# Where the weight sums of the token mixing are added: accumulating DMAs or VectorE

## The chip, the cores and the metric

The kernel runs on one core of a Trainium2 chip. The metric is device time in microseconds of one execution; the time before is the median of three runs. The engines named below are TensorE (PE in the profile, PEld for its weight loads), VectorE (DVE), ScalarE (ACT), GpSimd (POOL) and SyncE (SP), the last of which issues most DMAs.

## What is computed

One decoder layer on 512 tokens of width 1024, all in float32. Three sub-layers, each between RMS norms, with a residual:

```python
h = h + 0.5 * rmsnorm(swiglu(rmsnorm(h, ffn1_pre_w), ffn1_w_gu, ffn1_w_down), ffn1_post_w)
u = rmsnorm(h, mix_pre_w)
y = token_mixing(u, mem, w_in, ...)          # three branches, gated and summed, then w_out
h = h + rmsnorm(y, mix_post_w)
h = h + 0.5 * rmsnorm(swiglu(rmsnorm(h, ffn2_pre_w), ffn2_w_gu, ffn2_w_down), ffn2_post_w)
```

The token mixing projects u with w_in (1024 x 10240). Its columns feed a gated linear recurrence in chunks of 64 tokens (4 heads), a dilated sliding-window attention (3 groups of 4 heads), a cross-attention into 256 memory tokens (4 heads) and the gates of these three branches. Each branch's output goes through a 512 x 1024 matrix, is multiplied by its gate, and the sum goes through w_out.

## The kernel before

All of a stage's activations stay on the chip; the weights stream in from memory, and each is split into a high and a low float32r part (`wsplit`, `split`): ScalarE copies the high part (L161), VectorE subtracts it to get the low one (`tt`, L158). A product is then three matmuls: high by high, high by low, low by high.

Two column tiles of 128 columns, c1 and c2, are projected together, as a *pair*: a 2 x 2 block product in Strassen's manner, with seven block products in place of eight. The blocks of the weights are quarters of 512 rows by 128 columns: a11 and a12 (upper and lower half of c1), a21 and a22 (of c2). `wops` gives the seven operands: a11, a12, a22 and four sums:

- s1 = a21 + a22 (operand 5)
- s2 = s1 + a11 (operand 6)
- s3 = a21 + a11 (operand 7)
- s4 = s2 + a12 (operand 3)

`pair` takes the products in the order 1, 6, 5, 7, 2, 3, 4: twelve matmuls of 256 columns for each, 84 in all. At j = 6 it asks for s4 and with it for s2 and s1. `pairs` calls `wops`, which issues the loads, one pair ahead.

Loads: `load` brings a11 and a12 into one tile `st` (512 KB, four buffers). a22 goes into a tile named `sh` (256 KB, two buffers). The sums live in five buffers with the tag `sum`. In the kernel before, s1 and s3 are made by DMAs: the quarter a21 is loaded twice, once into each of two `sum` tiles (SP, L151), and POOL then issues a DMA that adds a22 to the one and a11 to the other (L302). s2 and s4 are VectorE adds (L309, through `tt`, so that the profile has them at L158).

Where the mixing has pairs: `hgrn_pair` (three pairs each for hg0 and hg1), `dil_pair` (six each for dil0 and dil1), mq0 and mq1 (one each), and `branch` (four for each of three branches), 32 in all. `ORDER` lists its steps. The two feed-forward stages (`ffn`) have 20 pairs each.

Order: the Python program gives the order of the work; attention steps are generators that `tick` resumes after so many microseconds of matmuls by the table `LAT`. A scheduler in the framework then lays down, when the program is built, the order of the instructions on each engine and each queue and gives out the tiles' buffers. At run time every engine takes its queue in order. Loads by `fetch` keep the order of the program; loads by `bring` are placed by the scheduler outside the first stage.

Of the kernel before, what the change touches and what calls it, by code (L numbers as in the profile page):

```python
# [12 lines left out]
ALU = mybir.AluOpType  # L13
# [4 lines left out]
P = 128  # L18
# [4 lines left out]
DFF = 2816  # L23
NF = DFF // P
# [28 lines left out]
class Layer:  # L53
# [228 lines left out]
                out += [(hi[:, i, :], lo[:, i, :]) for i in range(per)]  # L282
        return out

    def wops(self, w, c1, c2):

        st = self.load(w, 0, KD, c1, P)
        a11, a12 = st[:, 0:4, :], st[:, 4:8, :]  # L290
        a22 = self.stage.tile([P, 4, P], F32, tag="st2", bufs=2, name=f"sh{self.uid()}")
        quarter = lambda h: w.rearrange("(k p) c -> p k c", p=P)[:, 4 * h:4 * h + 4, c2:c2 + P]
        self.bring(a22, quarter(1))
        sums, ops = {}, {}

        def new_sum():
            return self.wpool.tile([P, 4, P], F32, tag="sum", bufs=NSUM, name=f"sum{self.uid()}")

        for n, x in (("s1", a22), ("s3", a11)):
            u = new_sum()  # L300
            self.bring(u, quarter(0))
            self.nc.gpsimd.dma_start(out=u, in_=x, accum_op=ALU.add)  # L302
            sums[n] = u

        def total(n):
            if n not in sums:
                a, b = {"s2": ("s1", a11), "s4": ("s2", a12)}[n]
                u = new_sum()
                self.tt(u, total(a), b, ALU.add)  # L309
                sums[n] = u  # L310
            return sums[n]

        def get(j):
            if j not in ops:
                if j == 6:
                    total("s4")
                ops[j] = self.wsplit({1: a11, 2: a12, 4: a22}.get(j) if j in (1, 2, 4) else total({3: "s4", 5: "s1", 6: "s2", 7: "s3"}[j]))
            return ops[j]
        return get

    def pairs(self, specs):

        ahead = None
        for x in specs:
            now, ahead = ahead, self.wops(*x)
            if now:
                yield now
        yield ahead
# [84 lines left out]
    def ffn(self, w_gu, w_down, w_post, ready, reload, after, chunks, early, plain):  # L413
# [3 lines left out]
        y = [[self.slot() for _ in range(2)] for _ in range(NT)]  # L417
        gw = self.col_tiles(w_gu, 0, plain)
        uw = self.col_tiles(w_gu, DFF, plain)
        pairs = self.pairs([(w_gu, f * P, DFF + f * P) for f in range(plain, NF)])  # L420

        def swiglu(sg, su, act):
            nc.scalar.activation(sg, sg, AF.Silu)
# [54 lines left out]
        for n in chunks:  # L478
            act = []
            for j in range(n):  # L480
                if before and 2 * j % n == 0:
                    ws = []
                    for i in range(0, before[1], 2):
                        ws += down_weights(before[0] + i, 2 * j // n)
                if f0 + j < early:
                    act.append(heads[f0 + j][1])
                else:
                    act.append(new_act())
                    if f0 + j < plain:
                        gu_plain([self.wcol(next(g)) for g in (gw, uw)], act[-1], slice(0, T))  # L490
                    else:
                        gu(next(pairs), act[-1])
                if before:
                    for i in range(8 * j // n, 8 * (j + 1) // n):
                        down(i % NT, i // NT, before[2], ws, before[0] == 0)
            before = (f0, n, act)
            f0 += n
# [236 lines left out]
    def dil_values(self, hd, s0, s12, st0, st1, v, out):  # L734
# [44 lines left out]
        for s in (s0, s12):  # L779
            pTs = []  # L780
            for i in range(2):
                tp = self.paux((P, 4, P))
                lo = 1 if (s is s0 and i == 0) else 0
                for j in range(lo, 4):
                    self.transpose(tp[:, j, :], s[i][:, j // 2, j % 2, :])
                pT = self.slot((P, 4, P))
                if s is s0:
                    nc.scalar.copy(pT[:, lo:, :], tp[:, lo:, :])
                else:
                    nc.vector.tensor_copy(out=pT, in_=tp)  # L790
                pTs.append(pT)
            yield LAT['dil3']
            po = self.paux((P, 4, P))
            for b in range(4):
                pT, j = pTs[b // 2], 2 * (b % 2)
                if s is s0:
                    pairs = [(v[0][b - 1], pT[:, j, :])] if b > 0 else []
                    pairs.append((v[0][b], pT[:, j + 1, :]))
                else:
                    pairs = [(v[1][b], pT[:, j, :]), (v[2][b], pT[:, j + 1, :])]  # L800
                for n, (vv, pp) in enumerate(pairs):
                    self.mm(po[:, b, :], vv[:, hs], pp, n == 0, n == len(pairs) - 1)
            if s is s0:
                nc.scalar.copy(y, po.rearrange("p a b -> p (a b)"))
            else:
                yv = y.rearrange("p (s a) -> p s a", a=4)
                self.tt(yv, yv, po.rearrange("p a s -> p s a"), ALU.add)
# [300 lines left out]
```

## Time and profile before

| what | value |
|---|---|
| three timed runs | 1394.15 us median (1392.47 to 1395.41) |
| the profiled execution | 1396.16 us |
| its span in the trace | 1394.4 us |
| instructions in it | 24579 |
| TensorE, VectorE, ScalarE, GpSimd busy | 1341.6, 1016.6, 744.5, 161.8 us |

Times in the trace count from the span's start. The busy time of TensorE is that of pipelined matmuls, each with a modelled end, so that it is not TensorE at its peak. "Idle before, and what ended it" names the instruction or DMA whose signal came last; "issue" stands there where the profile shows no such signal. The granted clock is the share of TensorE's full clock of 2.4 GHz.

By the trace the first feed-forward stage lasts until about 350 us, the mixing until about 1010 us; from about 1050 us on it is the second feed-forward stage.

### The profile page before, as it was taken

How to read it: one execution, taken by the hardware profiler on the slowest of the kernel's cores; microseconds unless marked ns; L12 is line 12 of the kernel's file. 1: busy time of each engine (PE TensorE's matmuls, PEld its weight loads, DVE VectorE, ACT ScalarE, POOL GpSimd, SP SyncE). 2: the span in 40 equal slices, each digit the busy share in tenths (PEclk: the TensorE clock that was granted, in tenths of full speed). 3: DMA queues.
4: the chain of work that ended last, by engine and by line, in shares of the span. 5: the costliest groups of instructions: out<-in, count | busy, mean ns of one | idle time of the engine just before them, and what ended most of it. 6: DMA issues, size and time to landing. Idle time of an engine off the chain costs nothing.

```text
span 1394.4 us, 24579 instructions
## 1 busy us (share of the span) xinstructions
PE 1341.6 (96%) x9197; PEld 1242.3 (89%) x9197; DVE 1016.6 (73%) x1932; ACT 744.5 (53%) x1527; POOL 161.8 (12%) x204
## 2 busy tenths in 40 slices
PE   6999999999999699998899999999999999999997
PEld 6999999999788688898889899999889999999995
DVE  6887777776888574576777787787569777767765
ACT  6675545554576464353655555555457655445541
POOL 1011110110200100111201201110010100100000
PEclk9999999999999899999899999999999999999998
DMA  9676565656536534576456656665365776655513
GB/s 269 141 185 180 137 151 148 158 143 179 175 96 178 150 106 136 148 184 150 103 126 149 166 127 160 154 163 131 111 219 145 175 181 160 150 145 140 149 46 136
DMA packets 264238, 210.95 MB, mean 151 GB/s; under 512 B 10645, under 2 KB 216886, under 8 KB 264118
## 3 DMA queue, kind: packets, MB, share of 16 engines
q1 hardware_dynamic: 242870, 171.56, 41.6%
q0 software_dynamic: 21248, 37.82, 16.4%
q8 instruction: 72, 1.18, 0.4%
q14 instruction: 48, 0.39, 0.1%
HBM read 162.12 MB, written 9.47 MB: 123 GB/s over the span
## 4 chain that ended last, share of the span: by engine, by line
PE 46%; DVE 3%; issue 2%; DMA 2%; ACT 0%; POOL 0%; DVEq 0%; POOLq 0%; ACTq 0%
PE ps L354 9%; PE ps L355 9%; PE ps L353 9%; PE ps L334 3%; PE ps L333 3%; PE ps L335 3%; PE px L340 2%; PE px L333 2%; PE px L334 2%; PE px L335 2%; DVE s L158 1%; DVE w L158 1%; PE px L344 1%; DMA sh<-in_w_in_dram 1%; DMA sum<-sh 1%
## 5 line engine op out<-in xcount | busy, mean ns | idle before, releaser
L161 ACT ACTIVATE w<-sum 128x512 fp32r<-128x512 f32 x288 | 180.1, 631 | 222.1 <-PE ps L354 174.9
L158 DVE TENSOR_TENSOR w<-sum,w 128x512 fp32r<-128x512 f32 x288 | 196.6, 689 | 87.1 <-ACT w L161 85.5
L353 PE MATMUL ps<-xhi,w 128*128 128x256 f32 x864 | 247.4, 286 | 0.9 <-ACT s L371 0.9
L355 PE MATMUL ps<-xhi,w 128*128 128x256 f32 x864 | 246.0, 285 | 0.7 <-DVE w L158 0.7
L354 PE MATMUL ps<-xlo,w 128*128 128x256 f32 x864 | 245.5, 284 | 0.0
L161 ACT ACTIVATE w<-st 128x512 fp32r<-128x512 f32 x260 | 163.5, 630 | 137.4 <-PE ps L354 97.1
L158 DVE TENSOR_TENSOR w<-st,w 128x512 fp32r<-128x512 f32 x260 | 177.3, 689 | 34.0 <-ACT w L161 32.1
L158 DVE TENSOR_TENSOR s<-s,s 128x256 f32<-128x256 f32 (+3 forms) x316 | 177.2, 566 | 19.0 <-ACT s L161 4.2
L353 PEld LDWEIGHTS ps<-xhi,w 128*128 128x128 f32 x864 | 166.7, 193 | 3.5 <-ACT s L371 1.1
L354 PEld LDWEIGHTS ps<-xlo,w 128*128 128x128 f32 x864 | 166.5, 193 | 2.5 <-issue 0.2
L355 PEld LDWEIGHTS ps<-xhi,w 128*128 128x128 f32 x864 | 166.8, 193 | 0.9 <-DVE w L158 0.9
L302 POOL DMA_DIRECT2D sum<-st x72 | 62.7, 871 | 642.9 <-DVE s L158 374.9
L158 DVE TENSOR_TENSOR sum<-sum,st 128x512 f32<-128x512 f32 x144 | 99.3, 690 | 46.0 <-issue 34.9
L158 DVE TENSOR_TENSOR s<-s,ps 128x256 f32<-128x256 f32 (+1 forms) x194 | 92.5, 478 | 33.5 <-PE ps L335 25.0
L333 PE MATMUL px<-s,s 128*128 128x512 f32 x288 | 112.6, 391 | 0.0
L334 PE MATMUL px<-s,s 128*128 128x512 f32 x288 | 112.5, 391 | 0.0
L335 PE MATMUL px<-s,s 128*128 128x512 f32 x288 | 112.0, 389 | 0.0
L302 POOL DMA_DIRECT2D sum<-sh x72 | 63.6, 883 | 301.2 <-DMA sh<-in_w_in_dram 101.5
L353 PE MATMUL ps<-t3hi,w 128*128 128x256 f32 x288 | 83.3, 289 | 0.5 <-DVE s L158 0.5
L353 PE MATMUL ps<-t4hi,w 128*128 128x256 f32 x288 | 82.0, 285 | 0.8 <-ACT s L374 0.8
L354 PE MATMUL ps<-t3lo,w 128*128 128x256 f32 x288 | 82.5, 286 | 0.0
L353 PE MATMUL ps<-t2hi,w 128*128 128x256 f32 x288 | 82.4, 286 | 0.0
(185 smaller groups left out, 3433.4 us busy)
## 6 DMA issues: line engine op xcount, KB each, us to landing
st<-in_ffn_w_gu_dram SPq DMA_DIRECT2D x48, 512.0 KB, 4.8
st<-in_w_in_dram SPq DMA_DIRECT2D x48, 512.0 KB, 4.2
st<-in_ffn_w_down_dram SPq DMA_DIRECT2D x44, 512.0 KB, 3.9
sum<-in_ffn_w_gu_dram SPq DMA_DIRECT2D x80, 256.0 KB, 3.3
sum<-sh POOLq DMA_DIRECT2D x72, 256.0 KB, 3.8
sum<-st POOLq DMA_DIRECT2D x72, 256.0 KB, 3.8
sum<-in_w_in_dram SPq DMA_DIRECT2D x64, 256.0 KB, 3.2
sh<-in_ffn_w_gu_dram SPq DMA_DIRECT2D x40, 256.0 KB, 3.5
```

What stands on the lines that cost most here:

```text
L158: self.pin(self.nc.vector.tensor_tensor(out=out, in0=a, in1=b, op=op))
L161: self.pin(self.nc.scalar.activation(hi, src, AF.Copy))
L302: self.nc.gpsimd.dma_start(out=u, in_=x, accum_op=ALU.add)
L333: mm(out, lhsT=lhs[0], rhs=rhs[0], start=first, stop=False)
L334: mm(out, lhsT=lhs[0], rhs=rhs[1], start=False, stop=False)
L335: mm(out, lhsT=lhs[1], rhs=rhs[0], start=False, stop=last)
L340: self.nc.tensor.matmul(out, lhsT=lhsT, rhs=rhs, start=start, stop=stop, **k)
L344: self.nc.tensor.transpose(out, in_, self.ident)
L353: mm(out, lhsT=lh, rhs=rh, start=first and k == 0, stop=False, skip_group_check=True)
L354: mm(out, lhsT=lh, rhs=rl, start=False, stop=False, skip_group_check=True)
L355: mm(out, lhsT=ll, rhs=rh, start=False, stop=k == 3, skip_group_check=True)
```

## The change

In the mixing, a21 is loaded once. VectorE adds s1 = a21 + a22 into a new `sum` tile when s1 is first asked for (at j = 6, before s2 and s4), and s3 = a21 + a11 in place in a21's tile when s3 is asked for (at j = 7). The feed-forward stages keep the two loads and the two accumulating DMAs.

```diff
-    def wops(self, w, c1, c2):
+    def wops(self, w, c1, c2, by_load):
...
-        for n, x in (("s1", a22), ("s3", a11)):
-            u = new_sum()
-            self.bring(u, quarter(0))
-            self.nc.gpsimd.dma_start(out=u, in_=x, accum_op=ALU.add)
-            sums[n] = u
+        if by_load:
+            for n, x in (("s1", a22), ("s3", a11)):
+                u = new_sum()
+                self.bring(u, quarter(0))
+                self.nc.gpsimd.dma_start(out=u, in_=x, accum_op=ALU.add)
+                sums[n] = u
+        else:
+            a21 = sums["a21"] = new_sum()
+            self.bring(a21, quarter(0))
 
         def total(n):
+            if n == "s3" and n not in sums:
+                total("s1")
+                self.tt(a21, a21, a11, ALU.add)
+                sums[n] = a21
             if n not in sums:
-                a, b = {"s2": ("s1", a11), "s4": ("s2", a12)}[n]
+                a, b = {"s1": ("a21", a22), "s2": ("s1", a11), "s4": ("s2", a12)}[n]
                 u = new_sum()
                 self.tt(u, total(a), b, ALU.add)
                 sums[n] = u
...
-    def pairs(self, specs):
+    def pairs(self, specs, by_load=False):
...
-            now, ahead = ahead, self.wops(*x)
+            now, ahead = ahead, self.wops(*x, by_load)
...
-        pairs = self.pairs([(w_gu, f * P, DFF + f * P) for f in range(plain, NF)])
+        pairs = self.pairs([(w_gu, f * P, DFF + f * P) for f in range(plain, NF)], True)
```

## Rows read from the trace of the kernel before

**Rows 1.** First page, totals: busy us, share of the span, instructions

```profile
PE 1341.6 (96%) x9197; PEld 1242.3 (89%) x9197; DVE 1016.6 (73%) x1932; ACT 744.5 (53%) x1527; POOL 161.8 (12%) x204
```

**Rows 2.** Busy time by stretch: length, busy (instructions) per engine, clock, DMA share, GB/s

```profile
core 0: us, PE busy (x) PEld busy (x) DVE busy (x) ACT busy (x) POOL busy (x), PEclk, DMA share, GB/s
...
455.00:490.00 35.00, 23.21 (x168) 22.40 (x167) 20.92 (x46) 16.24 (x38) 3.58 (x6) 0.80 0.53 137
...
590.00:668.00 78.00, 71.18 (x562) 69.53 (x561) 55.28 (x116) 37.37 (x89) 12.60 (x16) 0.97 0.71 169
...
777.00:795.00 18.00, 15.38 (x113) 14.80 (x113) 15.65 (x32) 10.93 (x31) 3.91 (x5) 0.91 0.75 181
795.00:980.00 185.00, 185.00 (x1313) 174.31 (x1313) 145.29 (x290) 108.65 (x209) 19.82 (x24) 1.00 0.58 144
```

**Rows 3.** Timeline of TensorE, rows after a wait: start, length, instruction, [idle before, releaser]

```profile
415.14 0.39 PE L355 MATMUL ps<-xhi,w 128*128 128x256 f32 x1 [0.71 <-DVE w L158]
...
466.02 1.09 PE L344 MATMUL px<-ident,s 128*128 128x128 f32 x4 [6.74 <-DVE s L190]
...
664.32 2.04 PE L340 MATMUL px<-s,s 128*128 128x128 f32 x8 [4.93 <-DVE s L158]
...
683.45 1.71 PE L340 MATMUL px<-s,s 128*128 128x256 f32 x4 [2.21 <-ACT s L575]
...
780.61 1.16 PE L340 MATMUL px<-s,s 128*128 128x128 f32 x8 [0.50 <-DVE s L158]
```

**Rows 4.** Busy time by stretch, columns as in rows 2, where the clock was low

```profile
663.40:670.20 6.80, 5.88 (x27) 5.92 (x28) 3.39 (x8) 5.09 (x20) 2.12 (x3) 0.50 0.41 120
...
789.70:793.10 3.40, 3.23 (x15) 3.26 (x16) 1.17 (x4) 2.63 (x7) 1.87 (x4) 0.50 1.04 257
```

**Rows 5.** Timeline of VectorE, 645 to 661 us, end of the first dil stage

```profile
645.67 1.42 DVE L158 TENSOR_TENSOR sum<-sum,st 128x512 f32<-128x512 f32 x2 [3.82 <-issue]
...
649.88 0.68 DVE L158 TENSOR_TENSOR w<-sh,w 128x512 fp32r<-128x512 f32 x1
...
652.10 1.30 DVE L158 TENSOR_TENSOR w<-sum,w 128x512 fp32r<-128x512 f32 x2
...
653.63 0.69 DVE L158 TENSOR_TENSOR w<-sum,w 128x512 fp32r<-128x512 f32 x1
657.66 1.42 DVE L158 TENSOR_TENSOR sum<-sum,st 128x512 f32<-128x512 f32 x2 [3.34 <-issue]
...
660.27 1.27 DVE L738 TENSOR_REDUCE st<-s 128x2 f32<-128x512 f32 x2
```

**Rows 6.** The queues beside it: SP, POOL, and landing of `sh` in 590 to 668

```profile
650.59 0.37 SPq L151 DMA_DIRECT2D sh<-in_w_in_dram  x1
...
654.34 0.85 POOL L302 DMA_DIRECT2D sum<-sh  x1 [8.98 <-DVE w L158]
...
DMA to landing us min/median/max: 3.1/3.4/8.0
```

**Rows 7.** Busy time by stretch, columns as in rows 2, two dil pairs

```profile
637.00:648.00 11.00, 10.74 (x90) 10.54 (x90) 7.15 (x14) 4.97 (x11) 1.69 (x2) 1.00 0.74 187
648.00:659.00 11.00, 10.01 (x82) 9.61 (x82) 7.59 (x15) 3.40 (x8) 1.69 (x2) 1.00 0.69 168
```

**Rows 8.** VectorE in 380 to 980: its waits for sums; the group of adds

```profile
DVE sum L158 <- issue: 27.5, 8, 5.0
...
L158 DVE TENSOR_TENSOR sum<-sum,st 128x512 f32<-128x512 f32 x63 | 43.5, 691 | 35.8 <-issue 27.5 <-DMA st<-in_w_in_dram 5.0 <-DMA sum<-sh 1.2
```

**Rows 9.** DMA issues, 380 to 980: queue, count, KB each, median us to landing

```profile
sum<-in_w_in_dram SPq DMA_DIRECT2D x60, 256.0 KB, 3.2
sum<-sh POOLq DMA_DIRECT2D x32, 256.0 KB, 4.1
...
s<-in_mem_dram SPq DMA_DIRECT2D x4, 256.0 KB, 7.4
```

## Prediction, before the changed kernel was run

> **What bounds the kernel now.** I read the first page of the profile, its engine totals, to begin with. TensorE is busy 96% of the span and VectorE 73% [rows 1]. A busy TensorE that is pipelined says little about lost time, so the second view was the table of stretches over the token mixing, which lies between about 380 and 1050 us. Outside a few short stretches TensorE is busy throughout: in the branch projections (795 to 980 us) for all of 185.0 us, with VectorE at 145.3 of 185 [rows 2]. There a weight sum can come earlier or later without any effect, as long as VectorE has room. TensorE's idle time lies in short stretches: 11.8 us in 455 to 490, 6.8 in 590 to 668 and 2.6 in 777 to 795 [rows 2], and a wait of 2.21 at 683 [rows 3].
>
> The third view was what ended TensorE's idle time there [rows 3]. The longest wait, 6.74 us at 466, ends with L190: that is the norm of the memory tokens, behind its own load, and has nothing to do with weight sums. Those at 415, 664 and 781 end with a VectorE step L158; the one at 683 with ScalarE's softmax. The wait before 664 (4.93 us) is followed by a stretch at half clock (0.50, that is 1.2 GHz) from 663.4 to 670.2; after the idle time before 790 the clock is at 0.50 from 789.7 to 793.1 [rows 4].
>
> The fourth view was VectorE's own order of time before that wait [rows 5]. At 645.67 and 657.66 it makes the adds s2 and s4 (two instructions, `sum<-sum,st`), after waits of 3.82 and 3.34 us that the profile calls "issue": nothing it shows released them. The queues tell what did [rows 6]. The load of the quarter a22 (`sh`) is issued at 650.59, as soon as VectorE has split the one before it (649.88); it takes 3.4 us (median here); POOL issues the accumulating DMA at 654.34, and VectorE starts 3.3 us after that. The add s2 thus stands behind a load and a second DMA that only starts once the load has landed, and everything later on VectorE's in-order queue stands behind s2. Per dil pair of 11 us VectorE works 7.15 and 7.59 us [rows 7]: with the wait it is full, 7.15 + 3.82 = 11.0. That is also what TensorE needs for a pair: of its 84 weight and 8 score matmuls it gets 90 into 11.00 us with 0.26 us idle [rows 7]. So VectorE, full because it waits, has nothing with which to make up the longer reductions at the end of the stage (660.27, [rows 5]), and TensorE stands still. In the mixing there are 8 such waits, 27.5 us in all [rows 8].
>
> **The change, part by part.** The mixing calls `pairs` at four places, all without the new argument: 6 hg pairs, 12 dil pairs, 2 mq pairs, 12 branch pairs, 32 in all. The 40 pairs of the two feed-forward stages pass True and keep their DMAs.
>
> Removed: 64 accumulating DMAs of 256 KB from POOL (4.1 us median to landing for those of `sh` [rows 9]) and 32 of the 64 loads of 256 KB into `sum` from SP (3.2 us [rows 9]). None of them is TensorE's work; what they are worth is what waits for them. POOL, which is in order too, issues 64 times less (0.85 us each, [rows 6]), and its later instructions (the power of the norms, the exchange of the softmax statistics) no longer queue behind an accumulate.
>
> Added: 64 VectorE adds, s1 = a21 + a22 and s3 = a21 + a11 (in place, safe on an in-order engine). An add of this form takes 691 ns [rows 8], but neighbours overlap: two that depend on each other take 1.42 us together [rows 5], which is 0.73 from start to start, and s1 is followed by s2, which depends on it; for s3 I take 0.60, the step between independent neighbours (two `w<-sum` in 1.30 us [rows 5], less 0.69). So 1.33 us a pair, 42.6 us on VectorE in all. [...]
>
> Moved: s3 is no longer ready before the pair but made just before its split; it needs only a21 and a11, which s1 and s2 needed before. The sums need four buffers of the five per pair, as now, but only one is held by a load in advance, so SP's in-order queue blocks less.
>
> Covered: in the branches VectorE has 39.7 us idle in 185 [rows 2] over 12 pairs, 3.3 us a pair, against 1.33 added: nothing on the path. If that cover failed, 12 times 1.33, 16 us, would be the price. The dil pairs have 11 - 7.15 = 3.85 and 11 - 7.59 = 3.41 us of VectorE without work [rows 7], now filled by the wait.
>
> What becomes of the wait is the unknown. The order on each engine is laid down by a scheduler when the program is built. If s1 stands where s2 stands now (behind the split at 653.63), a22 has landed by 650.59 + 3.4 = 654.0, VectorE is free at 654.3, and the wait is zero. If s1 is put directly behind the split at 649.88, the wait is the load's 3.4 us. The buffers of the sums are full at that point, and s1 can have one only when a sum of the pair before has been split (652.1 and later), so I take the lower half, about 1 us. Then VectorE needs 7.15 + 1.33 + 1 = 9.5 us per pair of 11 and keeps ahead.
>
> The sum, against the profiled execution's 1396.16 us (span 1394.4):
> - 590 to 668: of the 6.8 us idle [rows 2] I keep 1.6 for small waits at the score matmuls, which come with each of the pairs (0.50 at 781 is one, [rows 3]), and take off 5.2;
> - the half clock behind it: 5.88 us of TensorE work at half rate [rows 4], half of it lost, 2.9;
> - 777 to 795: 2.6 idle, less 0.4 that stays: 2.2; half clock over 3.23 us of work: 1.6;
> - the wait at 415: 0.7;
> - new: in the two stretches where TensorE waits for VectorE for other reasons (466, 683) one pair's adds can stand ahead of the awaited step: 2 times 1.33, +2.7.
>
> That is -12.6 + 2.7 = -9.9, so 1386.3 for a profiled execution. The three timed runs have their median 2.0 us below the profiled one: 1384.
>
> **The rivals.**
> A, the wait changes its name. s1 waits for the load as long as s2 waited for the accumulate, less what the adds take: the residual is about 2.2 us, VectorE is full again at 11 us, the stalls and half clocks stay, and the +2.7 remains or is absorbed. Time: 1394 to 1397. For it: TensorE's stalls hang on how late VectorE is, whatever made it late, and the a22 load is issued no earlier than now. Against it: the load has landed 3.3 us before VectorE now starts.
>
> B, slower. s1 is placed straight behind the split that frees a22's buffer. The wait is 3.4 us, and VectorE needs 7.15 + 1.33 + 3.4 = 11.9 us for a dil pair of 11: 0.9 us for each of 12, 10.6, and the 2.7 above: 1396.2 + 13.3 - 2.0 = 1407.5. It decides from a residual wait of 3.85 - 1.33 = 2.5 us upward. For it: VectorE is the busiest engine after TensorE and gets 42.6 us more. [...]
>
> C, more than forecast. With less DMA traffic the load of the memory tokens, 7.4 us to landing where a weight quarter of the same size takes 3.2 [rows 9], comes 4.2 us sooner, and so does the end of the 6.74 us wait; with POOL free of accumulates the statistics' exchange is early enough to take away the 2.21 at 683; and nothing is added on the path: 1384 - 4.2 - 2.2 - 2.7 = 1375. Against it: the share of DMA time is only 0.53 in 455 to 490 [rows 2].
>
> That the change does not do what it says is excluded by the code: the default of `by_load` is False, and both sums have one definition each.
>
> **How the numbers follow.** Forecast 1384: 0.52. C and what lies toward it: 0.16. A: 0.13. B, with half its price included: 0.19. The range reaches from just below C, 1373, over A to half of B's price, 1401, and leaves 0.05 below and 0.14 above. A measurement can tell about 0.2% from no change, 2.8 us: faster 0.67, same 0.13, slower 0.20.
>
> **What would show it.** Right: in the profile after, no `sum<-sh` or `sum<-st` from POOL in the mixing, 64 more adds of about 690 ns, VectorE's "issue" waits before the sums gone or near 1 us and named for the `sh` load, TensorE without a wait of 5 us at the end of the first dil stage, and no half clock there. Wrong: waits before the new adds of 2.5 us and more, or TensorE waits ending with L158 in the branches, where there are none now; then VectorE is the bound. The step that I am least sure of is where the scheduler puts s1. If it also moves TensorE's small matmuls, stalls can appear at places that no row here shows.

## The result, and the profile after

The changed kernel takes 1379.6 us (median of four runs, 1378.1 to 1381.8) against 1394.8 of the kernel before, a ratio of 0.9891 with the interval 0.987 to 0.9912: 15.2 us faster. The forecast was 1384 (10 us faster), the range 1373 to 1401. The profiled execution took 1379.57 us, right at the median (that of before was 2.0 above its own), with a span of 1377.8.

The engine totals of the page, as in [rows 1], and its lines on GpSimd's DMA queue and on memory:

```profile
PE 1335.2 (97%) x9197; PEld 1237.5 (90%) x9197; DVE 1051.6 (76%) x1996; ACT 743.6 (54%) x1527; POOL 107.0 (8%) x140
...
q0 software_dynamic: 12032, 21.04, 9.3%
...
HBM read 153.73 MB, written 9.47 MB: 118 GB/s over the span
```

VectorE has 64 instructions and 35.0 us more than before, GpSimd 64 instructions fewer. On q0 the page of before has 37.82 MB: the 16.78 MB less are the 64 accumulating DMAs of 256 KB. TensorE has the same 9197 matmuls.

Stretches that answer to [rows 2], with the same columns (times are earlier, since the kernel is ahead by then):

```profile
450.00:486.00 36.00, 27.61 (x200) 26.70 (x199) 25.10 (x54) 18.88 (x42) 2.01 (x3) 0.86 0.37 112
586.00:655.00 69.00, 68.31 (x559) 67.28 (x558) 62.05 (x127) 37.04 (x89) 2.12 (x4) 1.00 0.45 122
...
762.00:784.00 22.00, 21.08 (x173) 20.62 (x172) 19.47 (x45) 15.92 (x48) 3.93 (x6) 1.00 0.30 85
784.00:964.00 180.00, 180.00 (x1273) 169.39 (x1272) 149.87 (x295) 103.56 (x192) 1.79 (x2) 1.00 0.38 108
```

The first dil stage (586 to 655) now has 0.7 us of idle TensorE and a clock of 1.00, where it had 6.8 us and 0.97. VectorE is busy 62.05 of 69 us there, 90%, and TensorE still hardly waits: this is the forecast's main point. In the branches (784 to 964) TensorE is busy throughout, with VectorE at 149.87 of 180.

TensorE's timeline, rows after a wait, for [rows 3]:

```profile
460.63 0.63 PE L352 MATMUL px<-ident,s 128*128 128x128 f32 x4 [2.83 <-DVE s L190]
473.81 0.63 PE L352 MATMUL px<-ident,s 128*128 128x128 f32 x4 [3.57 <-DVE s L190]
...
652.97 1.13 PE L348 MATMUL px<-s,s 128*128 128x128 f32 x8 [0.52 <-DVE s L158]
...
670.35 1.13 PE L348 MATMUL px<-s,s 128*128 128x256 f32 x4 [1.64 <-ACT s L583]
...
774.32 1.13 PE L348 MATMUL px<-s,s 128*128 128x128 f32 x8 [0.20 <-DVE s L158]
```

The wait of 4.93 at the end of the first dil stage is 0.52, that of the memory tokens' norm (6.74) is 2.83, that of their softmax (2.21) is 1.64. No half clock follows the dil stages any more, nor the softmax, which before had 3.4 us of it from 683.9 on.

The clock of these views is a share. From one matmul's start to the next's (medians) it took 0.120 us for 256 columns and 0.227 for 512 at a share of 1.00, in both kernels: 2.4 columns a nanosecond for the 256 columns more. At 0.50, in the changed kernel, it took 0.213 and 0.427: 1.2 columns. The 2.4 and 1.2 GHz above are an estimate from these rates, with one column taken a cycle.

VectorE around the sums of one pair, for [rows 5] (`sum<-sum,sh` is the new s1; the `x2` holds s4 and s3). It is the last pair whose sums are made before TensorE reaches the end of the stage, and by the order of the pairs that is mq1: VectorE makes the sums more than a pair ahead of TensorE, which is at the last dil pair then.

```profile
643.43 0.69 DVE L158 TENSOR_TENSOR sum<-sum,sh 128x512 f32<-128x512 f32 x1 [1.21 <-DMA sh<-in_w_in_dram]
644.15 0.69 DVE L158 TENSOR_TENSOR sum<-sum,st 128x512 f32<-128x512 f32 x1
644.76 0.68 DVE L158 TENSOR_TENSOR w<-sum,w 128x512 fp32r<-128x512 f32 x1
...
646.30 1.41 DVE L158 TENSOR_TENSOR sum<-sum,st 128x512 f32<-128x512 f32 x2
```

And VectorE's waits for sums in the mixing (380 to 965 us; total, times, longest), for [rows 8]:

```profile
DVE sum L158 <- DMA sh<-in_w_in_dram: 5.2, 7, 1.6
```

27.5 us in 8 waits became 5.2 in 7, and what ends them is now named: the load of `sh`. Counting every wait before a sum, whatever ended it, 35.8 us became 7.3.

Where the time went can be read from the start of TensorE's n-th matmul in both traces, after minus before (both have 9197; a few matmuls changed places, so a step of under half a microsecond means nothing, and each trace is one execution):

| time in the kernel before | shift so far, us | what lies between |
|---|---|---|
| 100 | -2.1 | first feed-forward stage, whose pairs the change leaves alone |
| 379 | -2.6 | the rest of it |
| 390 | +0.3 | start of the mixing |
| 425 | -0.6 | the wait at 415 |
| 446 | -1.5 | |
| 467 | -5.9 | the memory tokens' norm |
| 487 | -4.4 | its second half |
| 648 | -5.4 | first dil stage |
| 672 | -14.0 | the end of that stage, with its half clock |
| 680 | -12.5 | |
| 686 | -14.1 | the memory tokens' softmax |
| 754 | -12.6 | second dil stage |
| 795 | -17.0 | the end of that stage |
| 850 | -16.0 | start of the branches |
| 1040 | -14.3 | branches, the mixing's end |
| end | -15.3 | |

The 2.9 us lost at the start of the mixing are a wait that the kernel before does not have, for a split of weights, with half clock from 379.3 to 382.7 behind it:

```profile
379.06 0.58 PE L342 MATMUL ps<-w,xhi 128*128 128x512 f32 x1 [1.81 <-DVE w L158]
```

### The profile page after: what moved, and what is told of

Its sections match the earlier page's. It is cut to its first block, busy times and chain, and to the rows that moved or that the text cites. A ratio compares the mean times of both kernels' runs of the same rounds, so it can differ in the third digit from the quotient of the medians.

```text
span 1377.8 us, 24355 instructions
## 1 busy us (share of the span) xinstructions
PE 1335.2 (97%) x9197; PEld 1237.5 (90%) x9197; DVE 1051.6 (76%) x1996; ACT 743.6 (54%) x1527; POOL 107.0 (8%) x140
## 3 DMA queue, kind: packets, MB, share of 16 engines
q0 software_dynamic: 12032, 21.04, 9.3%
## 4 chain that ended last, share of the span: by engine, by line
PE 79%; issue 8%; DVE 6%; DMA 3%; ACT 1%; POOL 1%; SPq 0%; POOLq 0%; DVEq 0%; ACTq 0%
PE ps L361 15%; PE ps L362 15%; PE ps L363 15%; PE ps L341 5%; PE px L341 5%; PE px L342 5%; PE px L343 5%; PE ps L342 5%; PE ps L343 5%; PE px L348 4%; DVE s L158 2%; DVE w L158 1%; PE px L352 1%; POOL r L181 1%; DMA s<-in_ffn_pre_w_dram 1%
## 5 line engine op out<-in xcount | busy, mean ns | idle before, releaser
L158 DVE TENSOR_TENSOR sum<-sum,st 128x512 f32<-128x512 f32 x176 | 120.2, 686 | 15.6 <-issue 9.4
L361 PE MATMUL ps<-t1hi,w 128*128 128x256 f32 x288 | 82.2, 285 | 0.0
L363 PE MATMUL ps<-t1hi,w 128*128 128x256 f32 x288 | 82.1, 285 | 0.0
L362 PE MATMUL ps<-t1lo,w 128*128 128x256 f32 x288 | 82.1, 285 | 0.0
```

What stands on the lines that cost most here:

```text
L158: self.pin(self.nc.vector.tensor_tensor(out=out, in0=a, in1=b, op=op))
L361: mm(out, lhsT=lh, rhs=rh, start=first and k == 0, stop=False, skip_group_check=True)
L362: mm(out, lhsT=lh, rhs=rl, start=False, stop=False, skip_group_check=True)
L363: mm(out, lhsT=ll, rhs=rh, start=False, stop=k == 3, skip_group_check=True)
```

## The experiments

The theories, as the expectations have them. **W**: TensorE's losses came from VectorE's waits before s2, for a load and an accumulating DMA in a chain; less traffic is worth nothing in itself. **T**: the gain comes from the traffic and the queue work that went (8.4 MB of loads, 16.8 MB of accumulating DMAs, 64 instructions on GpSimd), through loads and exchanges that land sooner. A third, rival B's worry, is that VectorE's added work costs on TensorE what it hides elsewhere. Gains below are one minus the ratio, times 1394.9, so the changed kernel's is 15.2; the intervals reach some 1.5 to 3.5 us to either side.

**1 and 2. The change in the 12 dil pairs alone, and in the 20 other pairs.**

The first:

```diff
-    def pairs(self, specs, by_load=False):
+    def pairs(self, specs, by_load=True):
...
-            pairs = self.pairs([(w_in, c, c + 512) for c in (C_DIL + g * 1536 + (2 * hp + i) * P for g in range(3) for i in range(2))])
+            pairs = self.pairs([(w_in, c, c + 512) for c in (C_DIL + g * 1536 + (2 * hp + i) * P for g in range(3) for i in range(2))], False)
```

The second leaves the default as it is and passes True in the last line.

> Only the 12 dil pairs get their sums from VectorE; the 20 other pairs of the mixing load a21 twice and accumulate by DMA as in the kernel before. Theory W (the gain is VectorE's wait for the accumulating DMA, which fills it in the dil stages): the two dil stage ends give back about 8 and 4 us, so 1394.8 - 12 = 1383 us. Rival T (the gain is lighter DMA traffic and a free POOL queue all over the mixing): the gain goes by the share of pairs, 12/32 of 15.2 = 5.7 us, 1389 us.

> The complement: VectorE makes the sums of the 20 hg, mq and branch pairs, the 12 dil pairs keep loads and accumulating DMAs. Theory W: only what happened before the dil stages stays, about 4 to 5 us at the memory tokens' norm and 1 us in hg0, so 1389 to 1391 us, with the wait of about 5 us at the end of the first dil stage and the half clock behind it still there. Rival T: 20/32 of 15.2 = 9.5 us, 1385 us.

Measured: dil alone 1384.4, ratio 0.9925 (0.9901 to 0.9949), 10.5 us gained; all but dil 1387.7, 0.9941 (0.9919 to 0.9964), 8.2. Together they are 18.7, with 15.2 for both at once, so they overlap in part. TensorE's waits, dil alone first, then all but dil:

```profile
464.06 1.09 PE L352 MATMUL px<-ident,s 128*128 128x128 f32 x4 [6.55 <-DVE s L190]
...
657.66 1.13 PE L348 MATMUL px<-s,s 128*128 128x128 f32 x8 [2.19 <-DVE s L158]
```

```profile
656.83 1.13 PE L348 MATMUL px<-s,s 128*128 128x128 f32 x8 [3.86 <-DVE s L158]
676.91 2.08 PE L348 MATMUL px<-s,s 128*128 128x256 f32 x4 [3.86 <-ACT s L583]
```

With dil alone the norm's wait (6.55) stays as it was and the dil stage's end is better; with all but dil the norm is better, and the softmax's wait at 677, which follows the dil pairs' DMAs, grows to 3.86. By place the first gives -5.4 and -4.4 us at the ends of the two dil stages, the second -3.9 at the norm, but also -3.7 and -3.1 at the ends of the dil stages, where W had expected nothing of it.

The reason is that the two runs do not separate what they were meant to. The waits at 645.67 and 657.66 in [rows 5] belong to the pairs mq0 and mq1, whose sums VectorE makes while TensorE is still at the dil pairs. So dil alone keeps the DMAs for them, and all but dil takes them away (VectorE's s2, s4 in the first, s1 in the second):

```profile
639.13 1.42 DVE L158 TENSOR_TENSOR sum<-sum,st 128x512 f32<-128x512 f32 x2 [1.97 <-DMA sum<-sh]
651.01 1.42 DVE L158 TENSOR_TENSOR sum<-sum,st 128x512 f32<-128x512 f32 x2 [2.90 <-DMA sum<-sh]
```

```profile
636.33 0.69 DVE L158 TENSOR_TENSOR sum<-sum,sh 128x512 f32<-128x512 f32 x1 [0.95 <-DMA sh<-in_w_in_dram]
647.32 0.69 DVE L158 TENSOR_TENSOR sum<-sum,sh 128x512 f32<-128x512 f32 x1 [0.96 <-DMA sh<-in_w_in_dram]
```

Both the six dil pairs and the two mq pairs thus lead up to the stall at the end of the first dil stage, and either change shortens it. Before the end of the second stage it is likewise the first pair of the branches (the wait of 4.57 us that ends at 777.1 in the kernel before). The dil ends are what the forecast was built on; the norm is not in its sum.

**3. The traffic put back, on the changed kernel.** The spare tile takes the loads and DMAs that the change removed; nothing reads it.

```diff
             self.bring(a21, quarter(0))
+            spare = self.slot((P, 4, P))
+            self.bring(spare, quarter(0))
+            for x in (a22, a11):
+                self.nc.gpsimd.dma_start(out=spare, in_=x, accum_op=ALU.add)
```

> The changed kernel plus the traffic that the change took away: each mixing pair loads a21 once more into a spare tile, and POOL adds a22 and a11 to it by DMA; nobody reads the spare tile. Theory W: VectorE does not wait for it, so the dil stages keep their gain (no wait over 2 us at their ends); the memory tokens' load meets the old traffic again and its wait goes from 3 back towards 6.7 us: about 1384 us. Rival T: the gain goes with the traffic, 1390 us and more.

Measured: 1408.4, ratio 1.0094 (1.0073 to 1.0116): slower than before. But it isn't a test of traffic: the added DMAs read `sh` and `st`, and those buffers can't be loaded anew until the DMAs are done, so VectorE waits for `sh` about as long as it had waited for the sums (37.1 us before all its sums, 35.8 in the kernel before; the longest wait 5.53, before 4.98), now with the added sums to make besides. Its group of s1 adds (count | busy, mean | idle before):

```profile
L158 DVE TENSOR_TENSOR sum<-sum,sh 128x512 f32<-128x512 f32 x31 | 21.4, 690 | 32.8 <-DMA sh<-in_w_in_dram 28.9 <-issue 2.7 <-DVE wt L158 0.9
```

Run 7 repeats it without holding the buffers.

**4. The kernel before with a22 in the slots' buffers and two more sums**, to let a22 come earlier and so to shorten the chain without moving any work to VectorE.

```diff
-NSUM = 5
+NSUM = 7
...
-        a22 = self.stage.tile([P, 4, P], F32, tag="st2", bufs=2, name=f"sh{self.uid()}")
+        a22 = self.slot((P, 4, P))
```

> The kernel before, accumulating DMAs and all, but with the buffers that hold its loads back widened: a22 comes from the general slots instead of two tiles of its own, and there are seven sum buffers instead of five, so that a22 can be loaded and accumulated earlier. No VectorE add is added. Theory W: if a22 lands some us earlier, VectorE finds the accumulate done, its waits before s2 fall from 3.5 to under 1 us, and the dil stage ends give back most of their 12 us: 1383 us; then the change's adds were not needed for the gain. If the waits stay at 3 us and more, the buffers were not what held the load. Rival T: the traffic is all there, so no gain, 1394 us.

Measured: 1526.4, ratio 1.0952 (1.0924 to 1.0981). The slots are shared with the activations, and the sums came later, not earlier. VectorE's waits over the whole span:

```profile
DVE sum L158 <- DMA sum<-s: 226.1, 51, 8.5
```

It leaves the wanted question open: an earlier a22 with the DMAs kept wasn't reached. Long waits in this place come with a longer time: 226.1 us of them stand beside 132.8 us more. How much of that they cause isn't shown, since other waits for slots may be in it.

**5 and 6. One sum each.** a21 loaded twice, as before; in 5 VectorE adds s1 and the accumulating DMA s3, in 6 the reverse.

The diff is that of 5; in 6 "s3" and a11 stand for "s1" and a22.

```diff
+            by_dve = {}
+            for n, x in (("s1", a22), ("s3", a11)):
+                u = new_sum()
+                self.bring(u, quarter(0))
+                if n == "s1":
+                    by_dve[n] = u
+                else:
+                    self.nc.gpsimd.dma_start(out=u, in_=x, accum_op=ALU.add)
+                    sums[n] = u
...
+            if n == "s1" and n not in sums:
+                u = by_dve[n]
+                self.tt(u, u, a22, ALU.add)
+                sums[n] = u
```

> In the mixing only s1 is made by VectorE (in place, in its own loaded quarter); a21 is loaded twice as before and s3 is still added by POOL's DMA. Theory W (what counts is that s2 no longer stands behind load, POOL and a second DMA): s1 is the sum that s2 waits for, so nearly the whole gain at the dil stage ends stays, 1380 to 1384 us, and VectorE's waits before the sums are near 1 us. If the gain needed both sums gone from POOL: half of it, 1387.

> The other half alone: in the mixing only s3 is made by VectorE, s1 by load and accumulating DMA as before. Theory W: VectorE still waits 3 us and more before s2, now with 0.6 us a pair more to do, so no gain at the dil stage ends: 1392 to 1396 us. Rival T (less traffic and POOL work): half of the gain, 1387 us.

Measured: s1 alone 1386.3, ratio 0.9956 (0.994 to 0.9972), 6.1 us gained; s3 alone 1395.8, 1.0018 (1.0002 to 1.0034), nothing gained. s3 alone leaves the chain of load and DMA ahead of s2, and the waits with it:

```profile
DVE sum L158 <- DMA sum<-in_w_in_dram: 16.5, 11, 6.0
DVE sum L158 <- issue: 10.1, 3, 3.9
DVE sum L158 <- DMA sum<-sh: 7.7, 4, 2.4
...
PE px L355 <- DVE s L158: 8.4, 6, 3.9
```

The waits for `sum<-sh` and "issue" are those of the chain ahead of s2: 17.8 us are left of them. The 16.5 us for `sum<-in_w_in_dram` are new: there VectorE waits for the second load of a21, to which it adds a11 for s3. So without s1 on VectorE there is no gain, as W says, but the run is not the kernel before with less traffic alone. TensorE's stall at the end of the first dil stage is still there (3.94 us, 6.8 us of half clock).

s1 alone should then have given nearly all, and gave 6.1 of 15.2. One half of what W asks for did not come about: VectorE's waits were to be near 1 us, and in the mixing 32.4 us of them are left, in 24 waits for `sh`, the longest 3.06. At the end of the first dil stage the run gains what the change gains (-8.3 us between 648 and 672, the change -8.6). At the end of the second it gains 0.8 of 4.4, behind two such waits of 3.06 and 2.04 us. And between them it loses 3.3 us:

```profile
673.12 2.08 PE L355 MATMUL px<-s,s 128*128 128x256 f32 x4 [5.27 <-ACT s L590]
```

The clock is at half from 670.0 to 676.8 there. This wait, for the memory tokens' softmax, is 1.64 in the changed kernel and 2.21 before. Ahead of it VectorE waited 4.46 us for the last exchange of the softmax statistics, which W does not have.

**7. Traffic put back without holding a buffer of the sums.** On the changed kernel: a spare slot is loaded with a21, and GpSimd accumulates a piece of the activations into it twice.

```diff
             self.bring(a21, quarter(0))
+            spare = self.slot()
+            self.bring(spare.rearrange("p (k c) -> p k c", k=4), quarter(0))
+            for i in range(2):
+                self.nc.gpsimd.dma_start(out=spare, in_=self.xhi[i][:, 0, :].bitcast(F32), accum_op=ALU.add)
```

> The changed kernel with the traffic of the kernel before put back beside it in a way that holds none of its buffers: each mixing pair loads a21 a second time into a spare slot, and POOL adds two pieces of the stage's input (which stays on the chip all through the mixing) to it by DMA; nobody reads the spare. The run before this one with traffic put back had these DMAs read a22 and a11, and the next loads of `sh` then waited for them. Theory W: the dil stage ends stay as in the changed kernel, VectorE's waits for `sh` at most 2 us, 1380 to 1386 us. Rival T: 1392 us and more, with `sh` landing as late as in the kernel before.

Measured: 1391.5, ratio 0.9983 (0.9969 to 0.9997): 2.4 us of the gain are left, though no wait for a sum is longer than 2.06 (14.4 us in all, 7.3 in the changed kernel). So with the chain ahead of s2 gone, transfers of this kind still take most of the gain away: neither W nor T alone has the whole of it. Three more runs ask which part of the transfers does it.

**9, 10 and 12. Only the load; only two DMAs from GpSimd, as plain copies; the load and the copies, with no accumulation.**

Run 9 is run 7 without its last two lines, and run 12 is run 7 without `accum_op`. The difference of run 10 from the changed kernel:

```diff
             self.bring(a21, quarter(0))
+            spare = self.slot()
+            for i in range(2):
+                self.nc.gpsimd.dma_start(out=spare, in_=self.xhi[i][:, 0, :].bitcast(F32))
```

> The changed kernel with one more load of the quarter a21 for each pair of the mixing, into a slot that nobody reads; no DMA from GpSimd. The run with this load and two accumulating DMAs from GpSimd lost 12 us of the gain of 15. If that loss is traffic from memory (loads that land later because 8 MB more are read), this kernel shows most of it: 1387 to 1392, with the loads of sh and sum landing later than 3.4 us. If the loss comes from GpSimd's queue (the exchange of softmax statistics behind the added DMAs) or from the accumulating DMAs themselves, the time stays near the changed kernel's: 1378 to 1382.

> The changed kernel with two DMAs of 256 KB from GpSimd's queue for each pair of the mixing, plain copies from an activation into a slot that nobody reads; no load more. If the loss of 12 us comes from GpSimd's queue and its transfers, this kernel shows most of it: 1387 to 1392, with the exchange of the softmax statistics issued later and TensorE waits behind it at the memory tokens' softmax (675) and near 810, as in the run with both. If it is traffic from memory: 1378 to 1382.

> The changed kernel with the extra load of a21 into a slot and, behind it, two plain copies from GpSimd's queue into the same slot: the run with two accumulating DMAs (1391.5 us), with the accumulation taken out and everything else as it was, the copies' wait for the load and for each other too. The extra load alone gave 1381.5 and the copies alone 1382.6, so the 12 us of that run are not their sum (about 5). If GpSimd's queue is what costs it (its DMAs wait for a load and hold up the exchange of the softmax statistics), this kernel has the same waits: 1389 to 1393. If it is the accumulation (an accumulating DMA takes the engines about twice as long as a copy of the same size, by the share of the queue: 7.2% of 1391.8 us for 64 against 3.4% of 1378.7), it gives about the sum of the two: 1382 to 1386.

| run | us | ratio, interval | lost of the 15.2 |
|---|---|---|---|
| 9, the load | 1381.5 | 0.9896 (0.9877 to 0.9914) | 0.7 |
| 10, two copies | 1382.6 | 0.9906 (0.9886 to 0.9926) | 2.1 |
| 12, load, then copies | 1388.5 | 0.9960 (0.9948 to 0.9972) | 9.6 |
| 7, load, then accumulates | 1391.5 | 0.9983 (0.9969 to 0.9997) | 12.8 |

Neither 8 MB more of loads nor 64 more DMAs cost much alone (0.7 and 2.1, each within its interval of nothing). Together, with each DMA behind its load, they cost 9.6, which is 6.8 more than the sum, and near what the expectation had for GpSimd's queue (1389 to 1393). The accumulation adds some 3, but those two intervals touch. The order laid down for the engines and for SP is the same in 7, 9 and 12: they differ on GpSimd's queue alone, and 7 and 12 only in the kind of DMA there. So the copies of 12, each behind a load, cost 7.1 us on top of that load.

Three places show it. At the end of the first dil stage the waits for `sh` grow. The last wait of the stage's s1 in 12, against 1.21 above:

```profile
647.59 0.69 DVE L158 TENSOR_TENSOR sum<-sum,sh 128x512 f32<-128x512 f32 x1 [2.30 <-DMA sh<-in_w_in_dram]
```

TensorE then waits 2.54 us at 657, with 3.4 us of half clock. 9 and 10 have 1.89 and 1.94 there, and TensorE waits 1.19 and 1.22, with no half clock. In these runs VectorE's room at the end of that stage thus runs out from about 2 us of waiting on, a little below the 2.5 at which rival B had it.

The second is the exchange of the softmax statistics on GpSimd's queue (`x<-st` writes them, `ot<-x` reads them back in another order). For the last of the stage in the kernel before, in the changed kernel and in run 12:

```profile
672.39 0.56 POOL L755 DMA_DIRECT2D x<-st  x1
674.16 0.89 POOL L302 DMA_DIRECT2D sum<-sh  x1 [1.21 <-issue]
674.71 1.12 POOL L758 DMA_DIRECT2D ot<-x  x1
```

```profile
660.79 0.56 POOL L763 DMA_DIRECT2D x<-st  x1
662.94 0.75 POOL L766 DMA_DIRECT2D ot<-x  x1 [1.59 <-DMA x<-st]
```

```profile
666.85 0.55 POOL L767 DMA_DIRECT2D x<-st  x1
668.84 0.54 POOL L311 DMA_DIRECT2D s<-xhi  x1 [1.45 <-DMA s<-xhi]
669.37 0.76 POOL L770 DMA_DIRECT2D ot<-x  x1
```

VectorE takes what comes back in `mm<-st,ot`, and behind that on its in-order queue stands the reduction of the memory softmax. In 12 and before, VectorE waits for it; in the changed kernel it doesn't:

```profile
673.23 0.16 DVE L158 TENSOR_TENSOR mm<-st,ot 128x4 f32<-128x4 f32 x1 [1.28 <-DMA ot<-x]
674.29 0.68 DVE L583 TENSOR_REDUCE mmx<-px 128x2 f32<-128x512 f32 x1
```

```profile
667.24 0.13 DVE L158 TENSOR_TENSOR mm<-st,ot 128x4 f32<-128x4 f32 x1
668.28 0.68 DVE L579 TENSOR_REDUCE mmx<-px 128x2 f32<-128x512 f32 x1
```

TensorE's wait for that softmax: 1.64 in the changed kernel and 1.65 in 1, 9 and 10, against 3.04 in 12, 3.32 in 7, 3.86 in 2 and 5.27 in 5, all four with DMAs that follow a load on GpSimd's queue there. In 10 the copies wait for no load, and none of them stands between this last `x<-st` and its `ot<-x`. The wait alone misleads, though: run 6 and the kernel before have such a DMA between the two as well, and wait only 1.74 and 2.21, because TensorE came late from the stall ahead of it. The time from the last score matmul of the dil stage to this one takes that out: 17.0 to 17.7 us in the changed kernel and in 1, 8, 9 and 10 (14.7 in 11), and 18.5 to 20.5 in the kernel before and in 2, 3, 5, 6, 7 and 12. That goes with the queue's order in all of them.

The third place comes behind the second dil stage, where the same exchange makes VectorE wait in 12:

```profile
795.39 0.17 DVE L158 TENSOR_TENSOR mm<-st,ot 128x4 f32<-128x4 f32 x1 [4.00 <-DMA ot<-x]
```

It is 4.24 us in 7, 2.76 in 10 and 3.25 in 9, and nothing in the changed kernel. Between 795 and 850 the lead falls by 4.1 us in 12 and 4.4 in 7, but by 3.4 and 2.9 in 9 and 10 as well, and by 1.0 in the changed kernel; DMAs behind loads are not needed for it.

How the 6.8 us split between these places isn't settled. The traces of 12 and 9 are one execution each, 3.6 us apart where the medians are 7.1 apart; by the start of the n-th matmul 12 falls behind by 2.9 us at the end of the first dil stage, by 2.2 between 467 and 487, and by only 0.2 between 672 and 686, around the softmax.

**8. The feed-forward stages too**, so that no accumulating DMA is left in the kernel.

```diff
-        pairs = self.pairs([(w_gu, f * P, DFF + f * P) for f in range(plain, NF)], True)
+        pairs = self.pairs([(w_gu, f * P, DFF + f * P) for f in range(plain, NF)], False)
```

> The changed kernel with the sums of the 40 feed-forward pairs made by VectorE too, so no accumulating DMA is left anywhere. In the first feed-forward stage of the changed kernel VectorE waits 4.7 and 3.4 us for sums at 59 and 80 us and TensorE 0.8 and 0.9 us at 62 and 64; behind that TensorE is never idle and VectorE has about 25% free. Theory W: those 1.7 us go and the 1.33 us a pair are covered: 1377 to 1380 us. If VectorE's 53 us more are not covered: 1385 us and more, with TensorE waiting for L158 in the feed-forward stages.

Measured: 1377.7, ratio 0.9883 (0.9858 to 0.9908). TensorE's waits at 62 and 65 us (0.64 and 0.77) are gone, but at 380 us it is where it was before: nothing that can be told from the changed kernel. In these stages the chain is covered.

**11. More work for VectorE.** The changed kernel with s1 added three times.

```diff
-                self.tt(u, total(a), b, ALU.add)
+                for _ in range(3 if n == "s1" else 1):
+                    self.tt(u, total(a), b, ALU.add)
```

> The changed kernel with s1 added three times over, two more VectorE adds of 691 ns for each pair of the mixing, 64 in all, some 39 to 44 us of VectorE work. If VectorE's cover is as wide as the prediction took it, the branches (some 3.3 us idle a pair before, 1.33 taken by the change) take 1.3 more without effect, and only the two dil stages, with 11 - 7.6 - 1.33 - 0.8 = 1.3 us left for each pair, come to the brim: 1380 to 1384. If VectorE is the bound already after the change, every pair gives back what is added, 1.33 times 32: near 1420; and the third add alone, in dil pairs only, would give 12 times 1.33, 1396.

Measured: 1381.4, ratio 0.9893 (0.9875 to 0.9912). Its totals:

```profile
PE 1334.9 (97%) x9197; PEld 1237.6 (90%) x9197; DVE 1085.5 (79%) x2060; ACT 743.5 (54%) x1527; POOL 107.1 (8%) x140
```

VectorE has 33.9 us more work, about as much again as the change gave it, and the time does not move by more than the intervals. The dil stages come near the brim (at their ends TensorE waits 1.69 and 1.07 us where it is 0.52 and 0.20 in the changed kernel), and the wait at the memory softmax goes from 1.64 to 0.2 in return. The part of rival B that prices the adds is excluded by this: as long as its waits are this short (3.3 us before all sums of the mixing), VectorE's adds cost little here. Its other part, waits of 2.5 us and more, did not come about in the changed kernel. Rival B's reason, that VectorE is the busiest engine after TensorE and gets more work, did not make the kernel slower: VectorE's occupancy goes from 73% to 76% and 79% while the time falls and stays.

## Why the prediction was right, and where it was not

- **The end of the first dil stage.** Forecast -5.2 of idle time and -2.9 of half clock, 8.1 together; the shift between 648 and 672 is -8.6, and the clock is 1.00. The waits that the prediction read there are gone, and run 6, which keeps the chain ahead of s2, keeps the stall. Whose waits they were the prediction had wrong: the two at 645.67 and 657.66 are those of mq0 and mq1, not of dil pairs. Runs 1 and 2 each give part of the gain (5.4 and 3.7), so that it can't be put on the dil pairs alone.
- **The end of the second.** Forecast -2.2 and -1.6; the shift between 754 and 795 is -4.4.
- **The wait at 415.** Forecast -0.7; measured -1.0 between 390 and 425. But run 1, whose pairs in that place keep their DMAs, has the same -1.0, so this isn't shown to come from the sums.
- **The residual wait.** Forecast about 1 us a pair, between 0 and 3.4. Measured 1.21 and less in the first dil stage, 1.63 and less in the second, 5.2 us over the 31 pairs of the mixing that the group of s1 adds shows.
- **The price of the adds.** Forecast 0.73 and 0.60 us from start to start; 643.43, 644.15, 644.76 above are 0.72 and 0.61. In all VectorE's busy time grew by 35.0 us, 0.55 an add, and not by 42.6. The adds are covered in the branches, as forecast, and in run 11 about twice as much is.
- **The +2.7 of adds ahead of awaited steps** is the term that was too small. It was to be 1.33 each at 466 and 683. The steps by which the lead falls come to 10.1 us: 2.9 at the start of the mixing, which the prediction did not name, 1.5 between 467 and 487, 1.5 between 672 and 680, 1.5 in the second dil stage, with a score wait of 1.61 at 734.7, and 2.7 from 795 to 1040. At the start of the mixing a VectorE add (374.34 us) stands ahead of the split that TensorE waits for, and a wait of 1.4 to 1.8 us is there in the changed kernel and in all runs in which VectorE adds s3 in the first pairs (2, 3 and 6 to 12), and in none of the others. At 1020 it is only the clock: a wait of 1.99 us, 1.94 before, is followed by 3.4 us of half clock in this execution. What makes the rest wasn't tried, and not all of it need be adds.
- **How near 1384 came is in part luck.** What the sum had too small on one side it lacked on the other: the norm below, 1.6 us at the softmax, whose half clock the sum did not have, and 2.6 us by which this execution is ahead at 379 us, before the mixing, without a changed pair.
- **What the sum left out** above all is the 4.4 us at the memory tokens' norm. The prediction said of this wait that it is "behind its own load, and has nothing to do with weight sums", and that is the step that failed. The place stood in rival C, with 4.2 us and a chance of 0.16, for the load that would land sooner. The landing was only part of it. The rows of the kernel before:

```profile
454.01 0.93 SPq L141 DMA_DIRECT2D s<-in_mem_dram  x2
...
463.64 0.86 POOL L302 DMA_DIRECT2D sum<-sh  x1 [8.43 <-ACT w L161]
464.20 0.89 POOL L181 TENSOR_TENSOR r<-v,mhalf 128x1 f32<-128x1 f32 x1
...
465.12 1.42 DVE L190 SCALAR_TENSOR_TENSOR s<-s,r,s 128x512 f32<-128x512 f32 x2 [1.23 <-POOL r L181]
```

and of the changed one:

```profile
451.27 0.93 SPq L141 DMA_DIRECT2D s<-in_mem_dram  x2
...
458.71 0.99 POOL L181 TENSOR_TENSOR r<-v,mhalf 128x1 f32<-128x1 f32 x1 [77.32 <-DVE v L180]
...
459.73 1.41 DVE L190 SCALAR_TENSOR_TENSOR s<-s,r,s 128x512 f32<-128x512 f32 x2 [0.44 <-POOL r L181]
```

The norm's last step starts 5.4 us sooner, and TensorE was 1.5 ahead there; the 3.9 between is the wait that went. SP issues the load 2.7 sooner (451.27 for 454.01), of which 1.5 is the lead: 1.2. The load lands 5.9 us after its issue, where it was 7.4 (the second of each pair): 1.5. And the power `r` on GpSimd, which stood behind the accumulating DMA of 463.64, starts as soon as its input is there: 1.2. Why SP issues it sooner isn't shown. The prediction had noted that GpSimd's later instructions (the power of the norms among them) no longer queue behind an accumulate, and then gave that no price. Run 1, with the DMAs kept in this place, has the full 6.55 of wait; run 2 without them has at most 3.0. Run 6 keeps an accumulate just ahead of the power and waits 5.87; in run 7 none of the added DMAs stands there (the first is issued at 462.71, the power at 460.32), and it waits 3.29.

- **Rival C's other pieces** came in part: the wait at 683 went from 2.21 to 1.64, not to nothing, and adds were paid for on the path. Of the 3.9 us at the norm 1.5 are the load that lands sooner, as it had them; the other 2.4 are the earlier issue of the load on SP's queue and the earlier start of the power on GpSimd's.
- **"None of them is TensorE's work; what they are worth is what waits for them"** was right, and incompletely followed. The statistics' exchange and the norm's power wait for them too, not only s2. Run 7 shows that this matters beyond s2's chain: with as many transfers back on the queues and that chain gone, 2.4 of the 15.2 us are left. It does not say how much each is worth, since its DMAs are others than those of the kernel before and the norm keeps its gain (3.7 of 4.4). Run 6 is the other side: with the chain kept, nothing is gained, though new waits for s3's load are in that.

## What to carry to other kernels

When a DMA that waits for a load stands on an in-order queue, list every later instruction on that queue and who waits for it; here a norm's power and an exchange of statistics stood behind the sums, and most of the gain came only where no such DMA was left on the queue and the sum's chain was gone, too. An engine at 73% that waits up to 4 us in a pair of 11 can be the bound, and the same engine with 35 us more work and no such wait is not: look at what it waits for before taking work from it. If two parts of a change each look cheap to undo (0.7 and 2.1 us here), undo them together before calling either harmless (9.6). When an experiment changes "one stage", check in the trace whose work runs there: an engine that works a pair ahead is in another stage than its neighbour.

## What was not expected of the hardware

An accumulating DMA within the chip took longer here than a copy of the same 256 KB: 4.5 us against 2.8 from issue to landing. The issues of runs 12 and 7 in the mixing (count, KB each, median us to landing):

```profile
s<-xhi POOLq DMA_DIRECT2D x64, 256.0 KB, 2.8
```

```profile
s<-xhi POOLq DMA_DIRECT2D x64, 256.0 KB, 4.5
```

(In run 10, where the copies wait for no load, it is 3.5.) GpSimd also took longer to issue it: 0.54 us for the copy at 668.84 above, 0.89 for the accumulating one at 674.16 (0.893 in the mean of the 64 of run 7). On the page the queue q0 (software_dynamic) moves the same 37.82 MB in 21248 packets and 16.5% of the engines' time in run 7, and in 17152 packets and 12.6% in run 12. Less the feed-forward stages' accumulates (12032 packets and 9.3% in the changed kernel) that leaves 7.2% for the 64 accumulates against 3.3% for the 64 copies, about twice as much. And the loads beside them landed later: the median of `sum` loads is 3.2 us in run 12 and 4.0 in run 7.
